# Pooling mixer of a two-layer decoder on one core: the two output tiles ahead of it, the mixer and the next squares as one list in an order kept by four engines

## Chip, cores and metric

The kernel runs on one core of a Trainium2 chip. The metric is the device time of one execution in microseconds (us), lower is better; it is given as the median of several runs. The engines are PE (TensorE, matmuls), DVE (VectorE), ACT (ScalarE), POOL (GpSimd) and SP (SyncE, which issues most loads).

## What is computed

One step of a decoder with two layers, for 512 prompt tokens and 8 sample tokens together (520 columns), all in float32, d_model 1024, d_ff 2816:

```python
x = x + 0.5 * swiglu(rms(x, g[l, 0]))           # every layer, first channel mixer
h = rms(x, g[l, 1])
x = x + (pool_mixer(h) if l == 0 else attention(h) @ w_o)
x = x + 0.5 * swiglu(rms(x, g[l, 2]))           # every layer, second channel mixer
y = rms(x, final_g)                             # at the end
```

The pooling mixer of layer 0 splits the 1024 features into four groups of 256. Group gi takes, for each token, the mean of the last 2, 4, 8 or 16 rows of h minus h itself, multiplies it by a 256x256 matrix and a scale per feature. The last 15 rows of h are outputs too (`pool_prompt`, `pool_sample`).

## The kernel before, in words

**Layout.** Features lie on the 128 partitions, tokens on the free axis: `x[k]`, k = 0 to 7, is 128x520. Every factor of a matmul is split into a rounded high part (by ACT, `hi`) and the rest (by DVE, `lo`), and each product is three matmuls: hi*hi, lo*hi, hi*lo. A split is thus always an ACT instruction, then a DVE instruction that reads its result.

**Weights.** `Weights` (L96) keeps a list of chunks (one DRAM load of up to 1 MB each on SP's queue into one of three `raw` buffers) and of items (a slice of a chunk, split into `wh`, `wl`, six buffers each). `get` hands out the next item, `prefetch` splits items five ahead. `hi` (L200) splits one item for a hand-written list: it returns `low`, the DVE half, and `ahead` (L219), which issues the load of the chunk two further on and then `add_up` for the next chunk. For a chunk that a Strassen tile uses, `add_up` calls `loaded` (L152): it loads a second copy `S` of 256 KB on SP and then starts two accumulating DMAs on POOL: `S<-raw` (L156), which needs `S` landed, and `raw<-raw` (L157). A new chunk can only be loaded when a `raw` buffer is free, that is when the last split of the chunk that held it is done. SP's loads are kept in the order of the program (`later`, L351).

**The channel mixer.** `ffn` (L672) computes hidden tiles, two plain ones (`plain_tile`, L577) and 20 by a Strassen scheme (`strassen_tile`, L614) in the case of the second one, and after each part of 8, 8 and 6 hidden tiles the eight output tiles m = 0 to 7. An output tile is 36 matmuls in the last part (`mm_tile`), `u` = result times 1/rms (DVE, L711), `x[m] -= u/2` (DVE, L712), and then, in the last part, `deferred` (L721): the split of g*x[m] for the next stage (xh, xl, L348 and L349), the square (ACT, L468) and its sum into `acc` (DVE, L472).

**The mixer** (L1006 to L1102). `zt(gi)` (L1013) multiplies the two feature tiles of a group by its matrix, in five parts tau: four blocks of 128 prompt tokens and one for the samples, six matmuls each. Parts 0 to 3 lie in one two-bank PSUM tile (`duo`, four such tiles exist), part 4 in another. `rstd_tok` (L477) sums `acc` over the partitions with five matmuls against a column of ones (L483) and computes 1/rms by 12 small DVE instructions (`root`, L486). `zt_evac` (L1031) takes every part out of PSUM, times 1/rms, as zh (ACT, L348) and zl (DVE, L349). `band` (L1038) multiplies zh, zl by the constant band matrices: 13 matmuls for each of the eight feature tiles m (L1052, L1060, L1061), then x[m] gets the result (L1062, L1065) and is split for the next channel mixer. The program is written as z0, norm, z1, evac 0, z2, evac 1, band 0, z3, evac 2, band 1, evac 3, band 2, band 3, then the eight squares and sums, then eight transposes for the 15 rows (L1095) and their copies (L1097). In what order the instructions go to the engines is decided by the framework's scheduler when the kernel is built.

**After it.** Behind the mixer, SP's queue has the copies of the state and of the caches (L1105, L1108: 0.4 and twice 1 MB) and 16 loads of sinks (L1114). The second `ffn` starts with two plain tiles; its `start_hooks` (L732) place `rstd_tok` behind the first of them and, around and after it, the combinations `sums` (L649) of g*x that the Strassen tiles need (xa, xb on ACT, L656; t on DVE, L661 to L667; th, tl, L345 and L346).

**Lists.** Three other stages (start, attention, end) are written as `Steps` (L237): each step has a name, an engine, an assumed cost, a due time, the steps it must follow (`after`), the buffers it takes (`takes`) and whose use frees them (`reads`). `order` plays the steps through: when an engine is free, the ready step with the earliest due time goes. The steps are emitted in the order of these start times inside `tc.manual_schedule`, which keeps that order on the engines named.

Of the kernel before, what the change touches and what calls it, by code (L numbers as in the profile page):

```python
# [18 lines left out]
P = 128  # L19
D = 1024  # L20
# [283 lines left out]
def yoco_step(ctx, tc, ins, outs):  # L304
# [27 lines left out]
    def ps():  # L332
        return duo()[:, 0, :]
# [117 lines left out]
        return gT[:, n * 8 + k : n * 8 + k + 1]  # L451

    N_KV, N_FIN, N_PS = 6, 7, 8
    r_tok = cp.tile([P, 8], F32, name="r_tok")
    R = cp.tile([P, TOK], F32, name="R")
    minus_half = cp.tile([P, 5], F32, name="minus_half")
# [9 lines left out]
    def square(k, pool, tag, order=lambda ins: ins):  # L466
        sq = pool.tile([P, TOK], F32, tag=tag, name="sq", bufs=1 if tag == "rp0" else 2)
        S.activation(sq, x[k], AF.Square)  # L468
        if k == 0:
            order(V.tensor_copy(acc[:, :TOK], sq))  # L470
        else:
            order(V.tensor_tensor(acc[:, :TOK], acc[:, :TOK], sq, op=ALU.add))  # L472
# [196 lines left out]
            split(tt[k + 4], t34)  # L669
            yield  # L670

    def ffn(fi, tmp, mov, hooks, tt, tags, after, before_last=None, given=None, end=None):  # L672

        j = 0
        for pi, n in enumerate(PARTS):
            last = pi == len(PARTS) - 1
            hs = Hidden(tags)
            for _ in range(n):
                if given is not None:
                    given(hs)  # L680
                    given = None
                elif j < NPL[fi]:
                    plain_tile(tmp, mov, hs, hooks)
                else:
# [8 lines left out]
            for m0 in range(0, KT, 2):  # L693
                banks = {m: duo() for m in (m0, m0 + 1)}
                if m0 == 0:
                    late = []
                    for m in (0, 1):
                        for k0, k1 in ((0, nk), (nk, n)):
                            w = W.get()
                            for k in range(k0, min(k1, n - 1)):  # L700
                                mm(w, k - k0, hs[k], banks[m], k == 0, False)
                            finish()
                        late.append((w, m))
                    for w, m in late:
                        mm(w, n - 1 - nk, hs[n - 1], banks[m], False, True)
                    W.prefetch()
                for m in (m0, m0 + 1):
                    if m0:
                        mm_tile(hs, banks[m])
                    u = tmp.tile([P, TOK], F32, tag="sb", name="u", bufs=nsb[0])  # L710
                    V.tensor_tensor(halves(u), banks[m][:, :, :H], halves(R), op=ALU.mult)  # L711
                    V.scalar_tensor_tensor(x[m], u, -0.5, x[m], op0=ALU.mult, op1=ALU.add)  # L712
                    if last:
                        if before_last is not None:
                            next(before_last, None)
                        after(m)

    def ff_pool():
        return tc.tile_pool(name="ff", bufs=2)

    def deferred(n, tmp, tag, tags, lst, w=TOK):  # L721


        def f(k):
            z = pair(tags, [P, w])
            split(tuple(a[:, :TOK] for a in z), x[k], gcol(n, k))
            lst.append(z)
            square(k, tmp, tag)

        return f  # L730
# [20 lines left out]
    with ff_pool() as tmp:  # L751
# [202 lines left out]
            return [step, norm, two, norm_all, two, step, step]  # L954

        prep = {}
        sel = cp.tile([P, 34], F32, name="sel")
        sts = cp.tile([P, KT, NS], F32, name="sts")

        def pool_prep():  # L960

# [44 lines left out]
    with tc.tile_pool(name="pm", bufs=2) as pm:  # L1006
        for k in range(KT):
            split(tuple(z[:, TOK:TW] for z in mov1[k]), sts[:, k, :])

        tok0 = (0, 128, 256, 384, 400)  # L1010
        r5 = pm.tile([P, 1], F32, name="r5", bufs=1)

        def zt(gi):  # L1013

            pd = duo()
            banks = [pd[:, 0, :], pd[:, 1, :], ps()]
            wh, wl = prep["w", gi]
            views = []
            for tau in range(5):
                o = banks[tau // 2][:, (tau % 2) * 256 : (tau % 2) * 256 + 256]  # L1020
                views.append(o)
                n = 0
                for kk in range(2):
                    xh, xl = mov1[2 * gi + kk]
                    s = slice(tok0[tau], tok0[tau] + P)
                    for a, b in ((xh, wh), (xh, wl), (xl, wh)):
                        T.matmul(o, a[:, s], b[:, kk, :], start=(n == 0), stop=(n == 5))  # L1027
                        n += 1
            return views

        def zt_evac(views):  # L1031
            zh = pm.tile([P, 5, 256], F32R, tag="zh", name="zh")
            zl = pm.tile([P, 5, 256], F32R, tag="zl", name="zl")
            for tau in range(5):
                split((zh[:, tau, :], zl[:, tau, :]), views[tau], r_tok[:, tau : tau + 1] if tau < 4 else r5)
            return zh, zl

        def band(gi, zz):  # L1038

            zh, zl = zz  # L1040
            Gt, (th, tl) = prep["G", gi], (prep["T", gi][:, 0, :], prep["T", gi][:, 1, :])
            G = lambda c: Gt[:, B_G + c : B_G + c + 256]
            for mi in range(2):
                m = 2 * gi + mi
                c = slice(mi * P, (mi + 1) * P)
                pd = duo()
                po, pso = pd[:, 0, :], pd[:, 1, :]
                pl = [(0, zh, th), (0, zl, th), (0, zh, tl), (1, zh, G(0)), (1, zl, G(0))]
                pr = [(1, zh, G(256)), (1, zl, G(256)), (2, zh, G(128)), (2, zl, G(128)), (3, zh, G(0)), (3, zl, G(0))]
                for half, lst in ((0, pl), (1, pr)):  # L1050
                    for i, (tau, z, b) in enumerate(lst):
                        T.matmul(  # L1052
                            po[:, half * 256 : half * 256 + 256],
                            z[:, tau, c],
                            b,
                            start=(i == 0),
                            stop=(i == len(lst) - 1),
                        )
                bs = Gt[:, B_S : B_S + NS]
                T.matmul(pso[:, :NS], zh[:, 4, c], bs, start=True, stop=False)  # L1060
                T.matmul(pso[:, :NS], zl[:, 4, c], bs, start=False, stop=True)  # L1061
                V.scalar_tensor_tensor(  # L1062
                    x[m][:, SP:], pso[:, :NS], gcol(N_PS, m), x[m][:, SP:], op0=ALU.mult, op1=ALU.add
                )
                V.scalar_tensor_tensor(  # L1065
                    x[m][:, :SP], po, gcol(N_PS, m), x[m][:, :SP], op0=ALU.mult, op1=ALU.add
                )
                z = pair(XX, [P, TOK])
                split(z, x[m], gcol(2, m))
                mov2.append(z)  # L1070

        mov2 = []
        hx = pm.tile([P, KT, P], F32, name="hx", bufs=1)
        for k in range(KT):
            S.activation(hx[:, k, 0:120], x[k][:, 400:520], AF.Copy, scale=gcol(1, k))
        z0 = zt(0)
        rstd_tok()
        z1 = zt(1)
        V.tensor_scalar(r5, r_tok[:, 4:5], sel[:, 32:33], sel[:, 33:34], op0=ALU.mult, op1=ALU.add)
        e0 = zt_evac(z0)  # L1080
        z2 = zt(2)
        e1 = zt_evac(z1)
        band(0, e0)
        z3 = zt(3)
        e2 = zt_evac(z2)
        band(1, e1)
        e3 = zt_evac(z3)
        band(2, e2)
        band(3, e3)
        for m in range(KT):  # L1090
            square(m, pm, "sq", later)
        for a in range(2):
            pt = ps()
            for k in range(4):
                T.transpose(pt[:120, k * P : (k + 1) * P], hx[:, a * 4 + k, 0:120], ident)  # L1095
            hrow = splp.tile([120, 512], F32, tag="S", name="hrow", bufs=4)
            S.activation(hrow, pt[:120, :], AF.Copy, scale=r_tok[:120, 4:5])  # L1097
            cols = slice(a * 512, (a + 1) * 512)
            nc.gpsimd.dma_start(pool_prompt[0, 0, :, cols], hrow[97:112, :])
            nc.gpsimd.dma_start(pool_sample[0, :, 14, cols], hrow[112:120, :])  # L1100

    movk = []  # L1102
    with ff_pool() as tmp:
# [853 lines left out]
```

## Time and profile before

| | us |
|---|---|
| three runs, median (lowest to highest) | 1675.85 (1675.25 to 1677.2) |
| the profiled execution | 1674.63 |
| its span, from the first to the last instruction | 1672.9 |

PE is busy in 98% of the span, DVE in 75%, ACT in 53%, POOL in 10%. The profile gives times within the span in us from its start; the mixer lies between 377 and 411. L-numbers are lines of the kernel; a name such as `ps` or `raw` stands for all its buffers. Matmul rows overlap: a matmul of 256 columns is shown with about 0.28 us, and one starts every 0.12 us.

### The profile page before, as it was taken

The numbers are of one execution on the slowest core, as the hardware profiler recorded it, in microseconds if no ns is written. First come the engines' busy times: TensorE is split into PE (matmuls) and PEld (weight loads), VectorE is DVE, ScalarE is ACT, GpSimd is POOL, SyncE is SP. The second block draws the span as 40 slices with busy tenths as digits, with TensorE's granted clock in tenths as the row PEclk, the third lists the DMA queues.
The fourth block names the chain that finished last, engine by engine and source line by source line (L and its number), as shares of the span: only waits on it lengthen the run. The fifth ranks groups of instructions, "written<-read, shape, count | busy, mean of one in ns | idle before, by whom it ended". The sixth has DMA issues, their size and how long they took to land.

```text
span 1672.9 us, 34562 instructions
## 1 busy us (share of the span) xinstructions
PE 1643.2 (98%) x13802; PEld 1625.0 (97%) x13802; DVE 1253.7 (75%) x2400; ACT 883.9 (53%) x1763; POOL 175.3 (10%) x235
## 2 busy tenths in 40 slices
PE   9899999999899999999999999999999999999997
PEld 9899999998899999999999999999989999999997
DVE  6865875887885785779785785778997785785786
ACT  6643643665662562556462463455875663463463
POOL 1101101100100100100110110100220110110100
PEclk9999999999999999999999999999999999999999
DMA  9446846653466666643765665644142575665641
GB/s 241 101 134 138 177 139 139 164 170 109 94 149 161 139 152 164 139 115 92 168 152 156 141 159 147 145 136 122 41 97 61 119 168 143 146 166 135 140 118 52
DMA packets 318240, 227.08 MB, mean 136 GB/s; under 512 B 9568, under 2 KB 293336, under 8 KB 318038
## 3 DMA queue, kind: packets, MB, share of 16 engines
q1 hardware_dynamic: 291360, 178.50, 38.1%
q0 software_dynamic: 23392, 41.83, 15.5%
q10 hardware_dynamic: 3326, 4.53, 0.9%
q8 instruction: 108, 1.77, 0.4%
q14 instruction: 54, 0.44, 0.1%
HBM read 180.89 MB, written 5.04 MB: 111 GB/s over the span
## 4 chain that ended last, share of the span: by engine, by line
PE 93%; DVE 4%; ACT 1%; issue 1%; DMA 0%; DVEq 0%; POOL 0%; ACTq 0%
PE ps L545 47%; PE ps L519 33%; PE pa L519 5%; PE ps L1778 2%; PE p L519 1%; PE pb L1383 1%; PE pc L1454 1%; PE pc L1439 1%; PE ps L1027 1%; DVE wl L193 1%; PE ps L1052 1%; DMA S<-raw 0%; DVE tl L346 0%; PE t L809 0%; ACT wh L192 0%
## 5 line engine op out<-in xcount | busy, mean ns | idle before, releaser
L192 ACT ACTIVATE wh<-raw 128x512 fp32r<-128x512 f32 (+1 forms) x690 | 418.2, 622 | 509.9 <-PE ps L519 295.0
L193 DVE TENSOR_TENSOR wl<-raw,wh 128x512 fp32r<-128x512 f32 (+1 forms) x690 | 456.4, 677 | 188.1 <-ACT wh L192 183.9
L545 PE MATMUL ps<-th,wh 128*128 128x260 f32 x1264 | 358.7, 284 | 4.1 <-ACT th L345 1.7
L545 PE MATMUL ps<-tl,wh 128*128 128x260 f32 x1264 | 358.1, 284 | 0.6 <-DVE tl L346 0.6
L545 PE MATMUL ps<-th,wl 128*128 128x260 f32 x1264 | 356.4, 284 | 1.0 <-DVE wl L193 1.0
L545 PEld LDWEIGHTS ps<-th,wh 128*128 128x128 f32 x1264 | 239.0, 189 | 5.6 <-ACT th L345 2.1
L545 PEld LDWEIGHTS ps<-tl,wh 128*128 128x128 f32 x1264 | 239.0, 189 | 1.0 <-DVE tl L346 1.0
L545 PEld LDWEIGHTS ps<-th,wl 128*128 128x128 f32 x1264 | 238.3, 189 | 1.5 <-DVE wl L193 1.5
L519 PE MATMUL ps<-hh,wh 128*128 128x260 f32 x1024 | 206.9, 283 | 0.6 <-ACT vtok L1205 0.6
L519 PE MATMUL ps<-hl,wh 128*128 128x260 f32 x1024 | 207.4, 283 | 0.0
L519 PE MATMUL ps<-hh,wl 128*128 128x260 f32 x1024 | 205.4, 282 | 0.0
L545 PE MATMUL ps<-xh,wh 128*128 128x260 f32 x708 | 199.6, 284 | 4.3 <-ACT wh L192 3.8
L545 PE MATMUL ps<-xl,wh 128*128 128x260 f32 x708 | 198.9, 283 | 0.0
L157 POOL DMA_DIRECT2D raw<-raw x79 | 68.4, 866 | 1242.1 <-DVE wl L193 556.3
L545 PE MATMUL ps<-xh,wl 128*128 128x260 f32 x708 | 195.4, 283 | 1.4 <-DVE wl L193 1.4
L519 PEld LDWEIGHTS ps<-hl,wh 128*128 128x128 f32 x1024 | 158.5, 189 | 0.0
L519 PEld LDWEIGHTS ps<-hh,wh 128*128 128x128 f32 x1024 | 157.1, 188 | 0.9 <-ACT vtok L1205 0.9
L519 PEld LDWEIGHTS ps<-hh,wl 128*128 128x128 f32 x1024 | 157.4, 188 | 0.0
L545 PEld LDWEIGHTS ps<-xh,wh 128*128 128x128 f32 x708 | 133.9, 189 | 5.2 <-ACT wh L192 4.4
L711 DVE TENSOR_TENSOR u<-ps,R 128x520 f32<-128x520 f32 x88 | 61.2, 696 | 98.4 <-PE ps L519 98.4
L545 PEld LDWEIGHTS ps<-xl,wh 128*128 128x128 f32 x708 | 134.0, 189 | 0.0
L545 PEld LDWEIGHTS ps<-xh,wl 128*128 128x128 f32 x708 | 131.9, 189 | 1.8 <-DVE wl L193 1.8
(299 smaller groups left out, 3241.3 us busy)
## 6 DMA issues: line engine op xcount, KB each, us to landing
raw<-in_ffn_w_gate_dram SPq DMA_DIRECT2D x87, 512.0 KB
raw<-in_ffn_w_up_dram SPq DMA_DIRECT2D x87, 512.0 KB
raw<-in_ffn_w_down_dram SPq DMA_DIRECT2D x32, 1024.0 KB
raw<-raw POOLq DMA_DIRECT2D x79, 256.0 KB, 3.3
S<-in_ffn_w_up_dram SPq DMA_DIRECT2D x79, 256.0 KB
S<-raw POOLq DMA_DIRECT2D x79, 256.0 KB, 4.7
raw<-in_ffn_w_down_dram SPq DMA_DIRECT2D x16, 768.0 KB
raw<-in_w_q_dram SPq DMA_DIRECT2D x8, 512.0 KB
```

What stands on the lines that cost most here:

```text
L157: G.dma_start(blk(raw, 2, 1), blk(raw, 1, 1), accum_op=ALU.add)
L192: nc.scalar.activation(dh, src, AF.Copy)
L193: nc.vector.tensor_tensor(dl, src, dh.bitcast(F32), op=ALU.subtract)
L519: T.matmul(banks[:, hf, :H], a[:, kk, :], hcols(b, hf), start=(first and i == 0), stop=(last and i == 2),)
L545: T.matmul(bank[:, :H], a[:, kk, :], b, start=(not more and kk == 0 and i == 0), stop=(kk == 3 and i == 2), skip_group_check=more,)
L711: V.tensor_tensor(halves(u), banks[m][:, :, :H], halves(R), op=ALU.mult)
L1027: T.matmul(o, a[:, s], b[:, kk, :], start=(n == 0), stop=(n == 5))
L1052: T.matmul(po[:, half * 256 : half * 256 + 256], z[:, tau, c], b, start=(i == 0), stop=(i == len(lst) - 1),)
L1383: T.matmul(o, q_[rows_, qc], k_[rows_, kc_], start=(i == 0), stop=(i == 2))
L1439: T.transpose(pt[:, o : o + P], vals["sm", t, h, bi][:, e, kt * P : (kt + 1) * P], ident)
L1454: T.matmul(po[rows_, bi * P : (bi + 1) * P], vtok[:, max(b - 1, 0) + kt, v0 : v0 + 64], vals["pp", t, h, bi][:, kt * 256 + e * P : kt * 25 ...
L1778: T.matmul(bank, a[:, k % 3, :], b[:, c0:c1], start=(k == 0 and i == 0), stop=(k == 5 and i == 2))
```

## The change

The first `ffn` stops after output tile 5 (`stop=6`). Output tiles 6 and 7, their splits, the mixer, its norm, the splits for the second channel mixer, the squares and sums for its norm and the transposes become one list of steps. `manual_schedule` names PE, DVE, ACT and POOL.

- The steps of `pool_prep` that went with output tiles 6 and 7 go, two each, with tiles 4 and 5. `sel` and `sts` are allocated earlier; the split of `sts` goes with each tile.
- The square of x[7] is no longer added to `acc` on DVE: `norm_sums` has ten matmuls in place of five (each column: `acc`, then the square). The 12 DVE instructions of `root` become one (`norm_mean`) and a power on POOL (`norm_root`).
- In the list, z0 to z2 are due ahead of the evacuations. The fifth parts of groups 0 and 1 share one bank of the tile in which the norm's sums are, those of groups 2 and 3 one bank of another tile.
- zh and zl lie in four pairs of 128x2x256 tiles of the hidden tiles' pool, one for parts 0 and 1 and one for 2 and 3, and small ones for part 4.
- Each band puts its halves into two banks and the samples beside the first; the result is added to x[m] by two DVE instructions as before.
- Items 0 to 8 of the weights are in the list (0 to 3 for output tiles 6 and 7, 4 to 7 the first hidden tile of the second `ffn`, 8 the first quarter of the second); five of them are split before the list begins.

The core of the diff:

```diff
-        ffn(0, tmp, mov0, first_hooks(), tt, HH, deferred(1, tmp, "g", XX, mov1, TW), pool_prep(), first_tile)
+        hs0 = ffn(0, tmp, mov0, first_hooks(), tt, HH, deferred(1, tmp, "g", XX, mov1, TW), pool_prep(), first_tile, stop=6)
+    with tc.tile_pool(name="pm", bufs=2, reuse_waits="tile") as pm:
+        first = W.ng
+        have = W.ns - first
+        st = Steps(dict(d=4, w=6, sq=2, u=2))
...
+        def w_lo(i):
+            lows.pop(i)()
+            aheads.pop(i)()
+
+        add("x5", "DVE", 3.0, -100.0)
+        add("y5", "ACT", 2.5, -100.0)
...
+        W_DUE = (0, 0, 2, 4, 33, 34, 37, 38, 42)
+        for i in range(9):
...
+                add(f"wh{i}", "ACT", 0.13 * n + 0.13, W_DUE[i], lambda i=i: w_hi(i), after=prev, takes=("w",))
+                add(f"wl{i}", "DVE", 0.14 * n + 0.13, W_DUE[i] + 0.1, lambda i=i: w_lo(i), after=[f"wh{i}"])
...
+            if n == 1 and m == 7:
+                nc.gpsimd.memset(q[:, TOK:], 0.0)
...
+                T.matmul(o, acc[:, lo : lo + P], ones[:, 0:1], start=True, stop=False)
+                T.matmul(o, vals["q", 1, 7][:, lo : lo + P], ones[:, 0:1], start=False, stop=True)
...
+        def norm_root():
+            nc.gpsimd.tensor_tensor(r_tok[:, :5], v, minus_half, op=ALU.pow)
...
+        def z_bank(gi, tau):
+            if tau < 4:
+                return vals["z", gi][:, tau // 2, (tau % 2) * 256 : (tau % 2) * 256 + 256]
+            return vals["f", gi // 2][:, 0, (gi % 2) * 256 : (gi % 2) * 256 + 256]
...
+            add(f"u{m}", "DVE", 0.7, d, lambda m=m: upd(m), after=[f"o{m}1"], takes=("u",), reads=[("d", f"o{m}0")])
+            add(f"x{m}", "DVE", 0.7, d + 0.1, lambda m=m: add_u(m), after=[f"u{m}"], reads=[("u", f"u{m}")])
...
+        for k in range(KT):
+            add(f"hx{k}", "ACT", 0.3, 9.0 + 0.1 * k, lambda k=k: h_part(k), after=[f"x{k}"] if k > 5 else ["y5"])
+        add("ns", "PE", 1.25, 10.5, norm_sums, after=["q7", "a6"], takes=("d",), reads=[("sq", "q7")])
+        add("nm", "DVE", 0.17, 11.0, norm_mean, after=["ns"], reads=[("d", "ns")])
+        add("nr", "POOL", 1.4, 11.0, norm_root, after=["nm"])
+        add("n5", "DVE", 0.28, 12.0, norm_r5, after=["nr"])
+
+        Z_DUE = (8.7, 12.3, 16.2, 19.5)
+        E_DUE = (13.5, 16.5, 19.5, 22.5)
+        B_DUE = lambda m: 23.5 + 1.8 * m
...
+                    f"eh{gi}{tau}", "ACT", 0.48, e, lambda gi=gi, tau=tau: z_hi(gi, tau),
+                    after=[f"z{gi}{tau}", "nr" if tau < 4 else "n5"] + first_e,
...
+                    f"ez{gi}{tau}", "DVE", 0.49, e + 0.5, lambda gi=gi, tau=tau: z_lo(gi, tau),
+                    after=[f"eh{gi}{tau}"], reads=[("d", holder)],
...
+            add(f"xp{m}", "DVE", 0.74, d + 1.5, lambda m=m: x_prompt_(m), after=[f"b{m}0", f"b{m}1", f"hx{m}"], reads=[("d", f"b{m}0")])
+            add(f"yh{m}", "ACT", 0.72, d + 2.3, lambda m=m: y_hi(m), after=[f"xs{m}", f"xp{m}"] + ([f"yh{m - 1}"] if m else []))
+            add(f"yl{m}", "DVE", 0.76, d + 3, lambda m=m: y_lo(m), after=[f"yh{m}"])
+            add(f"sq{m}", "ACT", 0.63, d + 12, lambda m=m: sq_of(2, m), after=[f"xs{m}", f"xp{m}", "ns"], takes=("sq",))
...
+        add("ht", "PE", 0.95, 30.0, h_turn, after=[f"hx{k}" for k in range(KT)], takes=("d",))
...
+        with tc.manual_schedule(
+            engines={mybir.EngineType.PE, mybir.EngineType.DVE, mybir.EngineType.Activation, mybir.EngineType.Pool}
+        ):
+            st.emit()
+        W.ng = first + 4
```

Steps are named o (output tile), u, x, q (square), a (sum), h and l (split of g*x), sh and sl (split of `sts`), ns, nm, nr, n5 (the norm), z (product of a group), eh and ez (its evacuation), b (band), xs and xp (result into x), yh and yl (split for the next channel mixer), sq and sa (square and sum for its norm), ht and ho (transposes and their copies), wh and wl (split of a weight item).

## Rows read from the trace of the kernel before

**Rows 1.** The page: span, busy shares, and the chain that ended last by engine.

```profile
span 1672.9 us, 34562 instructions
PE 1643.2 (98%) x13802; PEld 1625.0 (97%) x13802; DVE 1253.7 (75%) x2400; ACT 883.9 (53%) x1763; POOL 175.3 (10%) x235
PE 93%; DVE 4%; ACT 1%; issue 1%; DMA 0%; DVEq 0%; POOL 0%; ACTq 0%
```

**Rows 2.** Stretches: length; busy PE, PEld, DVE, ACT, POOL; granted clock; DMA share; GB/s.

```profile
378.00:384.00 6.00, 3.85 (x35) 3.68 (x33) 4.06 (x8) 2.59 (x7) 0.70 (x1) 1.00 1.03 296
386.00:388.00 2.00, 2.00 (x11) 2.00 (x11) 1.57 (x7) 1.05 (x3) 0.00 (x0) 0.50 0.91 295
437.00:450.00 13.00, 7.99 (x51) 6.33 (x50) 11.15 (x23) 8.77 (x17) 0.00 (x0) 1.00 0.01 2
```

**Rows 3.** Waits of PE, 360 to 452: us in total, times, longest.

```profile
PE ps L483 <- DVE acc L472: 2.2, 1, 2.2
PE ps L1052 <- DVE x L1065: 1.1, 1, 1.1
```

**Rows 4.** Chain of waits by time: start, us, what.

```profile
383.00 1.25 PE ps L483 x10
...
403.71 1.37 PE ps L1052 x11
...
405.20 1.35 PE ps L1052 x11
...
411.61 11.68 PE ps L519 x96
```

**Rows 5.** Timeline of PE: first and 24th matmul of z0.

```profile
377.13 0.29 PE L1027 MATMUL ps<-th,xh 128*128 128x256 f32 x1
...
379.87 0.28 PE L1027 MATMUL ps<-th,xl 128*128 128x256 f32 x1
```

**Rows 6.** Timeline of DVE, 359 to 428.

```profile
359.15 0.75 DVE L346 TENSOR_TENSOR bt<-pr,bt 128x256 fp32r<-128x256 f32 x2
...
371.85 0.68 DVE L712 SCALAR_TENSOR_TENSOR x<-u,x 128x520 f32<-128x520 f32 x1
...
376.24 1.28 DVE L193 TENSOR_TENSOR wl<-raw,wh 128x512 fp32r<-128x512 f32 x2
377.44 0.74 DVE L349 SCALAR_TENSOR_TENSOR xl<-x,gT,xh 128x520 fp32r<-128x520 f32 x1
378.11 0.68 DVE L711 TENSOR_TENSOR u<-ps,R 128x520 f32<-128x520 f32 x1
378.72 0.68 DVE L472 TENSOR_TENSOR acc<-acc,sq 128x520 f32<-128x520 f32 x1
...
386.50 0.17 DVE L498 SCALAR_TENSOR_TENSOR r_tok<-nt,ny 128x5 f32<-128x5 f32 x1
...
424.34 0.17 DVE L491 TENSOR_SCALAR nv<-ps 128x5 f32<-128x5 f32 x1 [1.57 <-PE ps L483]
```

**Rows 7.** Timeline of ACT: evacuation of group 2.

```profile
396.48 0.45 ACT L348 ACTIVATE zh<-ps,r_tok 128x256 fp32r<-128x256 f32 x1
396.83 0.46 ACT L348 ACTIVATE zh<-ps,r 128x256 fp32r<-128x256 f32 x1
...
398.34 0.47 ACT L348 ACTIVATE zh<-ps,r_tok 128x256 fp32r<-128x256 f32 x1
399.35 0.47 ACT L348 ACTIVATE zh<-ps,r_tok 128x256 fp32r<-128x256 f32 x1 [0.55 <-DVE zl L349]
400.38 0.47 ACT L348 ACTIVATE zh<-ps,r_tok 128x256 fp32r<-128x256 f32 x1 [0.55 <-DVE zl L349]
```

**Rows 8.** Timelines of SP and POOL, 376 to 386.

```profile
376.94 0.37 SPq L359 DMA_DIRECT2D raw<-in_ffn_w_gate_dram  x1
...
377.98 1.03 SPq L359 DMA_DIRECT2D S<-in_ffn_w_up_dram  x1
...
384.83 0.86 POOL L156 DMA_DIRECT2D S<-raw  x1 [0.67 <-DMA sink_s<-in_attn_sinks_dram]
```

**Rows 9.** The power on POOL in the last stage: ns min/median/max.

```profile
L1851 POOL TENSOR_TENSOR r_tok<-nv,minus_half x3: 543/696/1092, 1646.6 to 1666.1; 128x2 f32<-128x2 f32 x2, 8x1 f32<-8x1 f32 x1
```

More of the change, by code (lines that the diff above doesn't have):

```diff
@@ L670, in sums, with ffn @@
             yield
-    def ffn(fi, tmp, mov, hooks, tt, tags, after, before_last=None, given=None, end=None):
+    def ffn(fi, tmp, mov, hooks, tt, tags, after, before_last=None, given=None, end=None, stop=KT):
         j = 0
@@ L692, in ffn @@
                 break
-            for m0 in range(0, KT, 2):
+            for m0 in range(0, stop if last else KT, 2):
                 banks = {m: duo() for m in (m0, m0 + 1)}
@@ L715, in ffn @@
                             next(before_last, None)
+                            if stop < KT and m >= stop - 2:
+                                next(before_last, None)
                         after(m)
+        return hs
     def ff_pool():
@@ L1031, in zt_evac, with w_hi @@
[L1031 to L1040, printed above, removed]
+        hx = pm.tile([P, KT, P], F32, name="hx", bufs=1)
+        v = cp.tile([P, 5], F32, tag="nv", name="nv")
+        def w_hi(i):
+            lows[i], aheads[i] = W.hi()
@@ new lines, in out, with upd, add_u @@
+        def out(m, h):
+            if h == 0:
+                vals["o", m] = duo()
+            w = W.items[first + 2 * (m - 6) + h][2]
+            for k in range(3 * h, 3 * h + 3):
+                mm(w, k - 3 * h, hs0[k], vals["o", m], k == 0, k == 5)
+        def upd(m):
+            vals["u", m] = u = pm.tile([P, TOK], F32, tag="u", name="u")
+            V.tensor_tensor(halves(u), vals["o", m][:, :, :H], halves(R), op=ALU.mult)
+        def add_u(m):
+            V.scalar_tensor_tensor(x[m], vals["u", m], -0.5, x[m], op0=ALU.mult, op1=ALU.add)
@@ new lines, in z_part @@
+        def z_part(gi, tau):
+            if tau == 0:
+                vals["z", gi] = duo()
+            if gi == 2 and tau == 4:
+                vals["f", 1] = duo()
+            o = z_bank(gi, tau)
+            wh, wl = prep["w", gi]
+            n = 0
+            for kk in range(2):
+                xh, xl = mov1[2 * gi + kk]
+                s = slice(tok0[tau], tok0[tau] + P)
+                for a, b in ((xh, wh), (xh, wl), (xl, wh)):
+                    T.matmul(o, a[:, s], b[:, kk, :], start=(n == 0), stop=(n == 5))
+                    n += 1
@@ L1041, in band @@
+        def band(m, part):
+            gi, c = m // 2, slice((m % 2) * P, (m % 2 + 1) * P)
+            zh, zl = 0, 1
             Gt, (th, tl) = prep["G", gi], (prep["T", gi][:, 0, :], prep["T", gi][:, 1, :])
             G = lambda c: Gt[:, B_G + c : B_G + c + 256]
[L1043 to L1058, printed above, removed]
-                bs = Gt[:, B_S : B_S + NS]
[L1060 to L1070, printed above, removed]
@@ L1087, in yoco_step @@
[L1087 to L1095, printed above, removed]
+            if part == 0:
+                vals["b", m] = duo()
+                lst = [(0, zh, th), (0, zl, th), (0, zh, tl), (1, zh, G(0)), (1, zl, G(0))]
+            elif part == 1:
+                lst = [(1, zh, G(256)), (1, zl, G(256)), (2, zh, G(128)), (2, zl, G(128)), (3, zh, G(0)), (3, zl, G(0))]
+            else:
+                bs = Gt[:, B_S : B_S + NS]
+                lst = [(4, zh, bs), (4, zl, bs)]
@@ L1100, in yoco_step @@
             nc.gpsimd.dma_start(pool_sample[0, :, 14, cols], hrow[112:120, :])
+        for m in (6, 7):
+            d = 4.35 * (m - 6)
+            for h in range(2):
+                i = 2 * (m - 6) + h
+                before = [f"o{m}0"] if h else ["o61"] if m == 7 else []
+                add(
+                    f"o{m}{h}", "PE", 2.17, d + 2.17 * h, lambda m=m, h=h: out(m, h), after=[f"wl{i}"] + before,
+                    takes=() if h else ("d",), reads=[("w", f"wh{i}")],
+                )
+            d += 4.4
+            add(f"u{m}", "DVE", 0.7, d, lambda m=m: upd(m), after=[f"o{m}1"], takes=("u",), reads=[("d", f"o{m}0")])
+            add(f"x{m}", "DVE", 0.7, d + 0.1, lambda m=m: add_u(m), after=[f"u{m}"], reads=[("u", f"u{m}")])
+            late = 0.0 if m == 7 else 1.0
+            add(f"q{m}", "ACT", 0.63, d + 0.2 + late, lambda m=m: sq_of(1, m), after=[f"x{m}"], takes=("sq",))
+            if m == 6:
+                add("a6", "DVE", 0.7, d + 1.5, lambda: sum_of(1, 6), after=["q6", "x5"], reads=[("sq", "q6")])
+            add(f"h{m}", "ACT", 0.73, d + 0.5, lambda m=m: x_hi(m), after=[f"x{m}", "y5"])
+            add(f"l{m}", "DVE", 0.76, d + 1.0, lambda m=m: x_lo(m), after=[f"h{m}"])
+            add(f"sh{m}", "ACT", 0.19, d + 3, lambda m=m: s_hi(m), after=[f"h{m}"])
+            add(f"sl{m}", "DVE", 0.16, d + 3, lambda m=m: s_lo(m), after=[f"sh{m}"])
@@ new lines, in yoco_step @@
+        for k in range(KT):
+            add(f"hx{k}", "ACT", 0.3, 9.0 + 0.1 * k, lambda k=k: h_part(k), after=[f"x{k}"] if k > 5 else ["y5"])
[5 more added lines that the diff above has]
+        E_DUE = (13.5, 16.5, 19.5, 22.5)
@@ L1102, in yoco_step @@
+        add("ht", "PE", 0.95, 30.0, h_turn, after=[f"hx{k}" for k in range(KT)], takes=("d",))
+        for a in range(2):
+            add(f"ho{a}", "ACT", 0.6, 32.0, lambda a=a: h_out(a), after=["ht", "nr"], reads=[("d", "ht")])
+        with tc.manual_schedule(
[3 more added lines that the diff above has]
+        W.ng = first + 4
     movk = []
```

148 lines of the change are left out of this document (113 added, 35 removed).

## The prediction

> **What bounds the kernel now.** I read the page first. PE is busy in 98% of the span and carries 93% of the chain that ended last [rows 1]: time is gained only where PE stands still or runs slowly. The waits of PE around the mixer show where: 2.2 us for the last sum into `acc` before the norm, and 1.1 us in the bands for a result on DVE [rows 3]. Of the stretches, 378 to 384 has PE busy for 3.85 of 6 us, and 386 to 388 ran at a granted clock of 0.50, 1.2 GHz in place of 2.4, after that pause and the one-column matmuls of the norm [rows 2]. The chain gives the ends: the norm's matmuls begin at 383.0, the second channel mixer at 411.6 [rows 4]. The next stall is in 437 to 450, PE busy 7.99 of 13 while DVE is busy 11.15 [rows 2]; there the Strassen operands bind.
>
> The sum is made against the profiled execution: 1674.63 us, of which the span is 1672.9, 1.73 lying around it; the median of the runs, 1675.85, is 1.2 above it. From no change a measurement of this kernel tells 0.2%, 3.35 us.
>
> **The head of the list.** On PE, tiles 6 and 7 and then z0 stay where they are. Played through with its own costs, the list sends parts 0 to 3 of z0, then the norm's matmuls, z1, both fifth parts, z2, z3, the fifth parts of 2 and 3, the bands. A part is six matmuls at 0.119 us (24 from 377.13 to 379.87 [rows 5]), 0.71, so z0's four are done at 380.0.
>
> DVE, in order: x[5] ends at 372.5; after ACT's 0.73 follow its xl and sum, as in [rows 6], where an addition goes every 0.61 us (378.11 to 378.72) and an xl every 0.67 (377.44 to 378.11). That is 373.3 + 0.67 + 0.61 + 0.1 = 374.7. The list's order is then u6, x6, two weight splits (four times 0.61), xl6, a6 and a small one (1.36): 378.5; u7, x7: 379.7. The square (ACT, 0.6) ends at 380.4. PE waits 0.4 where it waited 2.2. Ten matmuls at 1.25/5 [rows 4] take 2.5, to 382.9: 1.25 more than before. The mean (0.17, as L491 [rows 6], and its latency) ends at 383.2. The power was 0.54 to 1.09 us on at most two columns [rows 9]; for five I take the upper one (bounds 0.7 and 1.4): **1/rms at 384.3 against 386.67** [rows 6].
>
> The moved steps of `pool_prep` cost nothing: the last ran at 359.15 [rows 6], long ahead of tile 4's end. The eight copies hx fill ACT's gaps before x6.
>
> **What stands ahead of the power on POOL.** `ahead` of item 8 issues the Strassen chunk B on SP and, for chunk A, the load of S and two accumulating DMAs on POOL. In the list's own play wl7 and wl8 go right behind x7, 2 us ahead of the power, and POOL is one of the engines whose order is kept. So POOL has: the small memset, `S<-raw`, `raw<-raw`, then the power; and behind the power wait all 20 evacuations on ACT.
>
> `S<-raw` waits for S to land. Before, B was issued at 376.94, just as wl7 ended (the first of two at 376.24), S at 377.98, and `S<-raw` could start at 384.83 [rows 8], 7.9 us after B's issue. Nobody waited for it: 1/rms was on DVE. Now wl7 ends at 379.7 + 0.6 = 380.3, B follows, and the same queue behind it (S, then the copies of state and caches) gives 380.3 + 7.9 = 388.2. Two DMAs of 0.86 [rows 8] and the power: **1/rms at 388.2 + 1.7 + 1.1 = 391.0**, 4.3 later than before. From below: wl7 cannot end before tile 7's last matmul (377.1), two additions and itself, 379.0; with S landing 6.85 after that (what S took from its own issue, as if B ahead of it cost nothing), the same two DMAs and the power in 0.7, 1/rms is at 388.3. From above, x7 a microsecond later and the power at 1.4: 392.3. I take 391.0, nearest to the measured queue. The state copies and sink loads behind it on SP shift by 3.4 us too; the next load on SP comes far later, so that costs nothing.
>
> **The evacuations.** In group 2, zh of a part starts 1.03 us after the previous part's (399.35, 400.38), each having waited for that part's zl; the fifth part went 0.35 after the first [rows 7]. So parts 0 to 3 of a group, in one two-bank tile, go one by one. The list assumes 0.48 per part and puts one group after the other on ACT, so four groups take 4 times (3 x 1.03 + 2 x 0.35) = 15.2 us, where the scheduler had two groups interleaved.
>
> The Trainium skill, page "PSUM — Partial Sum Buffer", section "PSUM bank collisions raise a hardware error", says that two engines have to be kept apart only on one bank and quadrant. By it part 2 would not wait for part 1 and the sum would be 2.8 us shorter; the trace disagrees, since part 2 (399.35), the first in its bank, waited 0.55 for part 1's zl [rows 7].
>
> **PE behind the norm.** z1, two fifth parts and z2 are ten parts, 382.9 + 7.1 = 390.0. z3 takes z0's tile, free when that is evacuated: 391.0 + 3.1 + 1.0 = 395.1. PE stands 5 us (if the clock falls behind the norm as before, that is hidden in it). Then z3, the fifth parts and bands 0 and 1 run to about 403; half clock after the pause can cost 2 us there, hidden behind the next wait: band 2 takes z3's tile, whose last evacuation ends at 391.0 + 3 x 3.8 - 0.35 + 3.1 + 1.0 = 406.1. Six bands at 1.49 (403.71 to 405.20 [rows 4]) and eight transposes at about 0.14: 406.1 + 8.9 + 1.1 = **416.1 against 411.6: 4.5 us later.** DVE after its last zl (407): x and yl of a band cost 0.15 + 0.66 + 0.67 = 1.5, PE's pace, so it keeps up, and the 1.1 us wait for x in the bands [rows 3] has no place of its own; the eight sums come last, 419 + 4.9 = 424, before PE asks for them at 416.1 + 11.7 = 428.
>
> **Downstream.** The first half of the next mixer is the same work. Before, DVE idled 1.57 us before that norm [rows 6]; now it idles more, and some Strassen sums may be pulled forward, shortening the stall in 437 to 450 by 0 to 1.5; a second drop of the clock may cost 0 to 1.7. I let the two cancel. **Sum: +4.5**, 1679.1 by the profiled execution, and on the median **1680.4**.
>
> **Rivals.**
> - *POOL is free* (the two DMAs do not stand ahead of the power, or S lands early; then that part of the list does what it says): 1/rms at 384.3, z3's last evacuation at 399.4, the second mixer at 409.4, 2.2 earlier: 1673.7; with sums pulled forward down to 1671. For it: before, `S<-raw` stood in nobody's way, and POOL is 10% busy [rows 1]. Against: the list keeps POOL's order, and wl8's place in it is early. It decides where S lands before 383.
> - *The stall swallows it*: the Strassen sums need x alone, so if they are put ahead of the norm, PE comes 5 us later to a stall of 5.0 us that has not moved: 1676. Against: before they ran behind the norm although x was there.
> - *Evacuation by banks*: only parts 1 and 3 wait, so a group takes 0.7 less, 2.8 in four; 1/rms still late: +4.5 - 2.8 = +1.7, 1677.6. Against: part 2's wait [rows 7].
>
> **Numbers.** Forecast 0.52 (+2 to +7.5: slower by over 0.2% in 0.42, within in 0.10). POOL free 0.25 (faster 0.13, within 0.12). Stall swallows 0.10, banks 0.08, both within. Another order elsewhere in the program, 0.05: faster 0.02, slower 0.03. Together faster 0.15, same 0.40, slower 0.45. The range leaves out a tenth below, in POOL free, and a tenth above, in the late landings: 1672.2 to 1683.4. The forecast's own is 1677.9 to 1683.4.
>
> **What would show it.** In the new trace: `S<-raw` on POOL between the memset and the power, the power's start after 387, the first zh 4 us later than 386.8; zh 1.03 apart; PE idle ahead of z3 and band 2; the second mixer's first matmul near 416. A power that starts at 383 proves the forecast wrong; zh 0.5 apart proves its second half wrong.

## The result, and the profile after

The changed kernel takes **1681.4 us** (median of 7 runs, 1679.32 to 1687.52) against 1675.85 of the kernel before: a ratio of 1.0044, 95% interval [1.0031, 1.0057], so slower by more than a measurement can miss. The ratio weighs all runs and is not the quotient of the two medians, which is 1.0033; two of the seven runs lie at 1686.71 and 1687.52. The profiled execution took 1681.4, 6.8 us more than that of before.

The page of the changed kernel, to be read against [rows 1]: span, busy shares, the chain that ended last by engine.

```profile
span 1679.6 us, 34572 instructions
PE 1645.9 (98%) x13812; PEld 1627.9 (97%) x13812; DVE 1251.2 (74%) x2388; ACT 883.7 (53%) x1763; POOL 177.9 (11%) x237
PE 89%; DVE 5%; ACT 3%; DMA 2%; issue 1%; SPq 0%; POOL 0%; DVEq 0%; ACTq 0%
```

The span is 6.7 us longer, and PE's share of the chain fell from 93% to 89%: DVE, ACT and DMA got it. Where, the chain of waits shows, cut to the steps that matter (start, us, what):

```profile
380.41 0.71 DVE x L1059
...
381.14 0.65 ACT sq L1078
...
382.82 1.22 SPq L359
...
386.42 2.63 DMA sraw<-in_attn_sinks_dram
389.04 0.07 POOL S L156
389.12 0.49 issue
389.61 1.26 POOL raw L157
390.87 1.25 POOL r_tok L1101
392.12 0.02 issue
392.14 0.85 ACT hh L1135 x2
...
401.90 3.81 PE ps L1123 x18
405.71 5.99 PE ps L1159 x52
411.70 0.95 PE ps L1184 x8
412.64 5.99 PE ps L1159 x52
418.63 1.43 PE ps L521 x11
```

The second channel mixer begins at 418.63 instead of 411.61 [rows 4], 7.0 us later, and that is all of the loss: from there to the end of the span it is 1261.0 us, before 1261.3. PE is not in this chain between 376 and 401.9; DVE, loads, POOL and the evacuations are.

POOL's timeline between the memset (361.52) and the power:

```profile
388.23 0.86 POOL L157 DMA_DIRECT2D raw<-raw  x1 [26.60 <-DMA sink_s<-in_attn_sinks_dram]
389.03 0.95 POOL L156 DMA_DIRECT2D S<-raw  x1
389.61 1.26 POOL L157 DMA_DIRECT2D raw<-raw  x1
390.18 1.93 POOL L1101 TENSOR_TENSOR r_tok<-nv,minus_half 128x5 f32<-128x5 f32 x1
```

SP's timeline, chunk B and S:

```profile
381.78 0.37 SPq L359 DMA_DIRECT2D raw<-in_ffn_w_gate_dram  x1
...
382.82 1.22 SPq L359 DMA_DIRECT2D S<-in_ffn_w_up_dram  x1
```

This is the picture of the forecast, with one DMA more: ahead of the power stand not only the two sums of chunk A but first `raw<-raw` of chunk B, which the scheduler had moved forward from behind the list. It needs B itself, and starts 6.45 us after B's issue; the mean had been there since 384.2. The name in brackets is the last DMA seen, a small load of sinks. That POOL waited for B is read from the times: in runs 1, 7 and 8 this DMA starts 6.33 to 6.37 us after B's issue, and before it was 6.36 (376.94 [rows 8] to 383.30). For it stood in the trace of before too, ahead of `S<-raw` at 384.83, in a row that [rows 8] leave out:

```profile
383.30 0.86 POOL L157 DMA_DIRECT2D raw<-raw  x1 [8.66 <-DMA sink_s<-in_attn_sinks_dram]
```

PE's waits from 376 to 420 (total, times, longest), against [rows 3]:

```profile
PE ps L1123 <- DVE hl L1139: 3.3, 1, 3.3
PE ps L1123 <- ACT hh L1135: 1.7, 1, 1.7
PE ps L1095 <- ACT sq L1078: 1.6, 1, 1.6
PE ps L1094 <- DVE xl L1074: 0.3, 1, 0.3
```

ACT's timeline, group 0 and the first two parts of group 1:

```profile
392.14 0.84 ACT L1135 ACTIVATE hh<-ps,r_tok 128x256 fp32r<-128x256 f32 x2 [9.36 <-POOL r_tok L1101]
393.53 0.48 ACT L1135 ACTIVATE hh<-ps,r_tok 128x256 fp32r<-128x256 f32 x1 [0.55 <-DVE hl L1139]
394.56 0.47 ACT L1135 ACTIVATE hh<-ps,r_tok 128x256 fp32r<-128x256 f32 x1 [0.55 <-DVE hl L1139]
...
395.29 0.84 ACT L1135 ACTIVATE hh<-ps,r_tok 128x256 fp32r<-128x256 f32 x2
```

Stretches of the changed kernel (columns as in [rows 2]):

```profile
378.00:384.00 6.00, 4.01 (x34) 3.75 (x33) 5.31 (x10) 3.88 (x10) 0.00 (x0) 1.00 0.15 40
386.00:388.00 2.00, 2.00 (x11) 2.00 (x11) 0.00 (x0) 0.00 (x0) 0.00 (x0) 0.50 1.48 449
396.00:404.00 8.00, 6.30 (x28) 6.00 (x29) 4.22 (x10) 3.90 (x10) 0.00 (x0) 0.50 0.45 111
444.00:457.00 13.00, 8.01 (x50) 6.36 (x49) 11.09 (x21) 8.26 (x16) 0.00 (x0) 0.97 0.01 2
```

The norm's stretch is no better than before, the first half clock (386 to 388, 1.2 GHz) is as before, and there is a second one, behind the wait ahead of z3, eight microseconds long. The stall of the Strassen operands is the same 8.01 of 13 us as before, only 7 us later.

From the first matmul of z0 to the second mixer it was 34.5 us before (377.13 to 411.61) and is 42.2 now (376.48 to 418.63), 7.7 more. PE's waits are 6.9 against 3.5 us: +3.4. Ten matmuls for the norm took 2.25 (nine starts from 381.83 to 383.86, and one earlier) against 1.1: +1.1. Half clock lost (length times one less the granted clock, in stretches of 2 us from 384 to 406, without the idle time) about 5.4 against 1.7: +3.7. That makes 8.2 for 7.7 measured, which is as near as such sums come.

### The profile page after: what moved, and what is told of

It is laid out like the page before. It is cut to its first block, busy times and chain, and to the rows that moved or that the text cites. A ratio compares the mean times of both kernels' runs of the same rounds, so it can differ in the third digit from the quotient of the medians.

```text
span 1679.6 us, 34572 instructions
## 1 busy us (share of the span) xinstructions
PE 1645.9 (98%) x13812; PEld 1627.9 (97%) x13812; DVE 1251.2 (74%) x2388; ACT 883.7 (53%) x1763; POOL 177.9 (11%) x237
## 3 DMA queue, kind: packets, MB, share of 16 engines
q1 hardware_dynamic: 291360, 178.50, 38.3%
## 4 chain that ended last, share of the span: by engine, by line
PE 89%; DVE 5%; ACT 3%; DMA 2%; issue 1%; SPq 0%; POOL 0%; DVEq 0%; ACTq 0%
PE ps L547 46%; PE ps L521 31%; PE pa L521 5%; PE ps L1947 2%; PE pb L1552 1%; PE pc L1623 1%; PE pc L1608 1%; PE ps L1159 1%; DMA pr<-in_bands_dram 1%; DVE wl L193 1%; DVE tl L346 0%; DMA S<-in_ffn_w_up_dram 0%; DMA S<-raw 0%; DMA raw<-in_ffn_w_gate_dram 0%; ACT wh L192 0%
```

## The experiments

All ten are built from the changed kernel. Runs 1 to 4, 5 to 8, and 9 and 10 form three groups, each on another chip. The runs of one group shared the runs of the kernel before, which had a median of 1674.83, 1674.79 and 1674.83 in the three groups; the ratios are to those, and that of the changed kernel is to the 1675.85 above. Times are medians; a trace is of one execution, and can lie a few microseconds from its kernel's median.

The first matmul of z0 lies between 375.0 and 377.4 in these traces, and the memset, far ahead of all that the edits touch, differs alike (359.6 to 362.4). So the last column, the time from z0 to the second mixer, compares traces better than the second mixer's own time; for the kernel before it is 34.5. From the second mixer to the end it is 1260.8 to 1263.2 us in every trace but that of run 10, where it is 1265.1.

| run | us | ratio [95%] | first evacuation | second mixer | z0 to it |
|---|---|---|---|---|---|
| changed kernel | 1681.4 | 1.0044 [1.0031, 1.0057] | 392.1 | 418.6 | 42.2 |
| power ahead of the sums | 1680.5 | 1.0029 [1.0018, 1.0039] | 385.8 | 414.6 | 38.3 |
| root on DVE | 1677.7 | 1.0007 [0.9996, 1.0019] | 386.2 | 410.1 | 35.1 |
| power ahead, groups in turns | 1676.8 | 1.0011 [1.0001, 1.0021] | 385.7 | 412.6 | 35.4 |
| root on DVE, groups in turns | 1677.0 | 1.0009 [0.9999, 1.0020] | 388.9 | 415.8 | 38.4 |
| reads behind the fourth part | 1679.6 | 1.0030 [1.0019, 1.0041] | 390.7 | 414.4 | 39.1 |
| both: power ahead, reads behind | 1675.2 | 1.0008 [0.9996, 1.0019] | 385.2 | 409.9 | 33.4 |
| these, norm behind z1, batches | **1671.8** | **0.9985 [0.9976, 0.9993]** | 386.5 | 407.5 | 31.4 |
| the same, power behind the sums | 1680.4 | 1.0033 [1.0020, 1.0045] | 391.9 | 414.5 | 38.1 |
| norm behind z1, no batches | 1675.4 | 1.0001 [0.9989, 1.0012] | 386.6 | 410.4 | 34.0 |
| batches, norm ahead of z1 | 1677.3 | 1.0009 [0.9997, 1.0021] | 387.5 | 412.6 | 35.2 |

**1. The power ahead of the three sums.**

```diff
 def w_lo(i):
     lows.pop(i)()
-    aheads.pop(i)()
+    if i != 8:
+        aheads.pop(i)()
...
+add("wa8", "-", 0.0, 12.0, lambda: aheads.pop(8)(), after=["nr", "wl8"])
```

> Edit: the changed kernel with the ahead part of weight split 8 (the two Strassen sums of chunk A, and with them the sum of chunk B that had come in ahead of them) made a step of the list that follows the power, so that the GpSimd queue runs memset, power, then the three sums. Nothing else moves; the loads of chunk B stay where they are in SyncE's order. Theory (the power is late only because it stands behind three accumulating DMAs that wait for chunk B and S to land): the mean at 384.04 us is followed by the power at once, 1/rms is there at 384.3 + 1.3 to 1.9 = 385.6 to 386.2 instead of 392.1, z3's tile is free before z2 is done (392.6), so the 3.3 us of idle ahead of z3 and the 1.7 us behind its third part go; the next mixer's first matmul comes at 410.5 to 413 instead of 418.6, and the time is 1673.5 to 1676 (the kernel before: 1675.85). Rival A (the list itself, with its evacuation chain of 3.2 us a group and bands behind all of z, costs the time): 1/rms comes early, but the next mixer still starts at 416 or later, time 1679 or more. Rival B (the stall at 444 to 457 waits for a load of fixed time, so an earlier start is swallowed there): next mixer by 413, idle from 444 to 457 grows from 5 to 10 us or more, time 1679 or more.

POOL's timeline, then two of PE's waits:

```profile
384.55 1.19 POOL L1102 TENSOR_TENSOR r_tok<-nv,minus_half 128x5 f32<-128x5 f32 x1 [23.53 <-DVE nv L1099]
387.54 0.92 POOL L157 DMA_DIRECT2D raw<-raw  x1 [1.81 <-DMA sink_s<-in_attn_sinks_dram]
```
```profile
PE ps L1124 <- ACT hh L1136: 2.0, 1, 2.0
PE ps L1096 <- ACT sq L1079: 1.6, 1, 1.6
```

The power follows the mean at once, 1/rms is there at 385.7, 6.4 us earlier, and the 3.3 us of idle ahead of z3 are gone: the queue was the cause of both. But the second mixer gained only 4.0 of them (414.6, where 410.5 to 413 was expected) and the time stayed at 1680.5. The half of the theory by which nothing else holds PE fell. Rival A's time came true, though its second mixer at 416 or later did not; and a piece of its cause was in plain sight, a wait of 2.0 us for ACT in the middle of z3, which the changed kernel also has, with 1.7. Rival B is out: PE is idle for 3.7 us of 440 to 453, not for 10. Of the 4.0 us this trace lost 2.2 again behind the second mixer (1263.2 us to the end against 1261.0); why stays open.

**2. The root on DVE.** The power replaced by the instructions of `root`, in the list at 2.3 us on DVE; POOL keeps its three sums where they are.

```diff
-nc.gpsimd.tensor_tensor(r_tok[:, :5], v, minus_half, op=ALU.pow)
+V.tensor_scalar(y.bitcast(I32), v.bitcast(I32), 1, None, op0=ALU.arith_shift_right)
...
-add("nr", "POOL", 1.4, 11.0, norm_root, after=["nm"])
+add("nr", "DVE", 2.3, 11.0, norm_root, after=["nm"])
```

> Edit: the changed kernel with the power on GpSimd replaced by the eleven small VectorE instructions that the kernel before used (shift, subtract, three Newton steps), in the same place of the list; the GpSimd queue keeps its three sums where they are. Theory (queue behind the sums): 1/rms is there 2.4 us behind the mean, as in the kernel before (384.28 to 386.67), so at 386.5; first evacuation on ScalarE at 386.8; no wait ahead of z3; next mixer's first matmul 411.5 to 414, time 1674.5 to 1677, about 1 us behind the run that only reorders the queue. Rival A (the list itself): next mixer 416 or later, 1679 or more. Rival C (the power is slow in itself, whatever stands ahead of it): this run reaches 1676 and the reordered queue does not.

1/rms came 2.4 us behind the mean (383.76 to 386.2) and the second mixer at 410.1, earlier than expected, but z0 began 1.5 us earlier too, so that from z0 it is what was expected; the traced execution took 1673.12, the median was 1677.7, a little above the range. By the order of the two times alone rival C would fit. The traces speak against it: in the first run the power took 1.19 us, and 1/rms was there 1.2 us behind the mean's end, sooner than here. What made this run better is the list: with 2.3 us assumed for the root, `order` put group 3's reads behind z3's fourth part, that part carries no wait for ACT any more, and PE stands still nowhere inside z3. That led to run 5.

**3 and 4. Evacuations of two groups in turns**, with the power ahead and with the root on DVE.

```diff
-E_DUE = (13.5, 16.5, 19.5, 22.5)
+E_DUE = (13.5, 13.75, 19.5, 19.75)
```

> Edit: the reordered queue of the first run, and the evacuations of groups 0 and 1, and of groups 2 and 3, ordered in turns (part 0 of group 0, part 0 of group 1, part 1 of group 0, ...) by their due times, so that consecutive evacuations read different two-bank tiles. Theory that the split of a part (ScalarE's high half, then VectorE's low half) is serialised inside a tile, 1.03 us a part where 0.84 us for two were seen: the twenty evacuations take about 10.5 to 11 us instead of 13; but from 386 on TensorE has z1's rest, z2, z3 and the bands in front of it without a gap, so at most 0 to 1.5 us of it shows: next mixer 409.5 to 412, time 1673 to 1675.5. Rival D (evacuations are not on the path at all once 1/rms is early): same as the first run within 0.2%, and no row of TensorE waits for hl or hh.

> Edit: the VectorE root of the second run with the evacuations in turns of the third. Theory: as the second run, less what the turns take off the path: 1673.5 to 1676. Rival D: as the second run within 0.2%.

Neither reached its range (1676.8 and 1677.0). The evacuations did get shorter: in run 3 the last nine parts of groups 0 and 1 left from 388.69 to 392.91, 0.47 each. But with these due times the third and the fourth part of z3 both wait for a read of the tile, and PE stood still twice in the mixer after the norm, 2.0 us (run 3) and 1.7 us (run 4) in all. Run 4 is level with run 2, as rival D has it, and run 3 is faster than run 1. The two runs don't tell the theories apart, because the due times changed more than one thing.

**5. Reads only behind the fourth part**, with POOL as the change has it.

```diff
-after=[f"z{gi}{tau}", "nr" if tau < 4 else "n5"] + first_e,
+after=[f"z{gi}{max(tau, 3)}", "nr" if tau < 4 else "n5"] + first_e,
```

> Edit: the changed kernel with one more condition in its list: a part of a group is read by ScalarE only after the fourth part of that group is written (the first run still had TensorE waiting 2.01 us for ScalarE's hh in the middle of z3, at 397.8, where z3's fourth part is issued behind reads of the same two-bank tile; the changed kernel waits 1.70 us there). The power stays behind the three sums, so 1/rms stays at about 392. Theory (second cause: TensorE's write into a tile waits for earlier reads of another part of that tile): the wait of 1.70 us goes, z3 to z34 run as 36 matmuls without a gap from 396.0, and the next mixer starts 2 to 3.5 us earlier, at 415 to 416.6, time 1677.5 to 1679.5. Rival (the wait only moves to the next evacuation, so the order of reads is indifferent): next mixer at 418 or later, time 1680 or more.

PE's only wait from 386 to 404 in its timeline:

```profile
394.54 0.58 PE L1123 MATMUL ps<-th,xh 128*128 128x256 f32 x1 [3.35 <-DVE hl L1139]
```

The 1.7 us inside z3 are gone, those ahead of z3 stay: the second cause is real and separate. In the program the fourth part of z3 carries a wait on ACT, because in the changed list a read of another part of the same two-bank tile comes earlier; with the new condition that wait is not there. From z0 to the second mixer it took 3.1 us less, within the 2 to 3.5 expected; the time, 1679.6, is at the upper end of its range. The ratio went from 1.0044 to 1.0030, a step that the two intervals do not tell from none.

**6. Both at once.**

> Edit: both at once, the power ahead of the three sums (first run) and the reads of a group behind its fourth part. Theory (two causes, the queue and the order inside z3, that hid each other: the first run took 1/rms from 392.1 to 385.7 and the next mixer only from 418.5 to 414.5, with 2.01 us of wait inside z3): no wait of TensorE inside z3, next mixer 410.5 to 412.5, time 1673.5 to 1676, that is, no slower than the kernel before. Rival (TensorE's half clock, 382.3 to 389 in the first run, is what is left, and sets it): next mixer 413 or later, time 1677 or more.

Nothing waits inside z3, the second mixer starts at 409.9, a little earlier than expected, 1675.2: level with the kernel before. Of the way from z0 the first cause alone gave 3.8 us, the second 3.1, both together 8.8. By the ratios it is 0.0015, 0.0014 and 0.0036, of which only the last is clear of noise. The half clock ahead of it (0.50 at 384 to 386) did not keep it from that, so the rival is out as the thing that is left; it is still a cost, as run 10 shows.

**7. The norm's sums behind four parts of z1, and evacuation in batches.**

```diff
-add("ns", "PE", 1.25, 10.5, norm_sums, after=["q7", "a6"], ...)
+add("ns", "PE", 1.25, 10.5, norm_sums, after=["q7", "a6", "z13"], ...)
...
-    after=[f"eh{gi}{tau}"], reads=[("d", holder)],
+    after=[f"eh{gi}{max(tau, 3)}"], reads=[("d", holder)],
```

> Edit: as the second of this call, and the sums of the norm follow the first four parts of z1 (TensorE stood idle for 1.64 us behind the first sum, waiting for the square), and VectorE's low halves of a group follow all four high halves of it, so that ScalarE and VectorE read different tiles. Theory: no idle time on TensorE between z0 and the bands but up to 1 us ahead of z3; if the half clock at 382 to 389 came from that idle time, it goes with it; bands from about 394, next mixer 407 to 410, time 1669 to 1673, 0.1 to 0.3% below the kernel before. Rival (the clock falls whatever TensorE does there): half clock stays at 382 to 389, next mixer 410 to 412, time 1673 to 1675.5.

ACT's timeline (first two groups), PE's waits, and two stretches:

```profile
386.48 1.57 ACT L1136 ACTIVATE hh<-ps,r_tok 128x256 fp32r<-128x256 f32 x4 [4.24 <-POOL r_tok L1102]
387.92 0.49 ACT L1136 ACTIVATE zh<-ps,r 128x256 fp32r<-128x256 f32 x1
388.28 1.60 ACT L1136 ACTIVATE hh<-ps,r_tok 128x256 fp32r<-128x256 f32 x4
```
```profile
PE ps L1124 <- DVE hl L1140: 0.8, 1, 0.8
PE ps L1124 <- DVE nv L1099: 0.3, 1, 0.3
```
```profile
378.00:384.00 6.00, 6.00 (x55) 6.00 (x54) 5.08 (x10) 3.33 (x9) 0.00 (x0) 1.00 0.25 70
384.00:388.00 4.00, 3.75 (x31) 3.55 (x31) 0.44 (x2) 1.52 (x5) 1.63 (x2) 1.00 1.19 340
```

Four parts leave in 1.6 us, a group in 1.8, PE stands still for 1.0 us in all from z0 to the second mixer, and in this trace it is at full clock all that way: the second mixer at 407.5, 4.1 us ahead of the kernel before (3.1 counted from z0), **1671.8 us, ratio 0.9985**. This beats both kernels. That the clock stays up because the idle time is gone, as the theory has it, is not shown: it fell in runs 8 and 9, which have the norm in the same place.

**8. The same with the power behind the sums.**

> Edit: the third of this call with the power put back behind the three sums, as the change has it. Theory (the queue costs what it delays 1/rms by, once nothing else holds z3): 1/rms at about 392, TensorE idle for 5 to 7 us ahead of z3 and at half clock behind it, next mixer 413.5 to 416, 5 to 8 us behind the third run; time 1676 to 1679. Rival (the list's order alone made the change slow): within 2 us of the third run.

One wait of PE, one stretch:

```profile
PE ps L1123 <- DVE hl L1139: 4.6, 1, 4.6
```
```profile
384.00:388.00 4.00, 3.74 (x22) 3.55 (x22) 0.17 (x1) 0.00 (x0) 0.00 (x0) 0.64 1.30 376
```

This is the cleanest pair: one step of the list apart, 414.5 against 407.5 (6.7 us counted from z0), and 8.6 us apart by the medians (ratio 1.0033 against 0.9985). The time, 1680.4, is above the range given. In a list in which nothing else holds z3, the queue costs 7 us of the way to the second mixer. The clock differs too: here it fell at 385, in run 7 it did not, though PE's work up to there is the same.

**9 and 10. The two halves of run 7 apart.**

> Edit: the run that beat both kernels (1671.78 us) with VectorE's low halves put back in turns with ScalarE's high halves; the power is ahead of the three sums and the norm's sums follow four parts of z1. Theory: in turns a group takes ScalarE 3.2 us, with batches 1.8 us (first groups 386.48 to 388.28), so group 3 is read some 4 us later; the third band waits for it, and the next mixer starts 1 to 2.5 us later than 407.39, at 408.5 to 410, time 1673 to 1674.5. Rival (the order of the evacuation does not show, the norm's place alone gave the gain): next mixer within 0.5 us of 407.39, time within 0.5 us of 1671.78.

> Edit: the run that beat both kernels with the norm's sums put back ahead of z1; the power is ahead of the three sums and the evacuations stay in batches. Theory: TensorE stands idle for 1.64 us behind the first sum again, and the half clock behind it costs 1.5 us more as in the run with the queue and the whole tiles (382 to 388); bands no earlier than 396, next mixer 409 to 410, time 1673.5 to 1675.5. Rival (what is idle ahead of 1/rms is covered, the evacuation alone gave the gain): next mixer within 0.5 us of 407.39.

Without batches (run 9) the second mixer starts at 410.4, 2.9 later (2.7 from z0; a little more than expected), and what waits is the third band. PE's timeline, and a stretch:

```profile
400.28 0.36 PE L1160 MATMUL ps<-bt,hh 128*128 128x256 f32 x1 [1.65 <-DVE x L1163]
```
```profile
386.00:388.00 2.00, 2.00 (x13) 2.00 (x12) 0.76 (x2) 0.84 (x2) 0.78 (x2) 0.53 1.30 407
```

DVE's last low half of z3's parts ended at 400.14, and the small x that the profile names went right behind it; PE's work follows both. The half clock of that trace lies ahead of this wait, which hides it: from 386 to 400 no evacuation of ACT waits for a matmul. Without the move of the norm (run 10) it is 412.6 (3.9 later from z0), later than expected: PE waits 1.64 us for the square and runs at half clock for the 4 us that follow it, and for two more, to 390. The traced execution was one of the longer ones, 1679.88 where the median is 1677.3. The stretch:

```profile
384.00:388.00 4.00, 4.00 (x20) 4.00 (x21) 0.93 (x4) 0.47 (x2) 1.19 (x1) 0.50 1.11 288
```

Both rivals are out: each half is needed for the time of run 7. The medians, 1675.4 and 1677.3 against 1671.8, lie above what was expected too.

## Why the prediction was right, and where not

Sign and chief mechanism were right: 1680.4 forecast, 1681.4 measured. The size was too low: +4.5 forecast, against +5.6 by the medians, +6.7 by the two spans and +7.0 at the second mixer, and that the medians lie 1 us apart is partly luck. A range from 1672.2 to 1683.4, which holds a gain as well as a loss, was easy to meet; what the traces bear out are the steps. By these:

- **The queue ahead of the power: right, with a DMA missed.** The forecast had two DMAs ahead of the power, the trace three. B was issued at 381.78 (forecast 380.3), since x7 came at 381.1 and not at 379.7; `S<-raw` then started 7.25 us after it (forecast 7.9), the first DMA at 388.23 (forecast 388.2, as it happens). 1/rms came at 392.1 against 391.0: B was 1.5 later, `S<-raw` 0.65 sooner behind it, and from `S<-raw` to 1/rms it was 3.1 where 2.8 was forecast. What the third DMA cost no run shows, for none takes it out. The power itself is 1.19 us where POOL is free (run 1), 1.25 in the chain here: the 1.1 taken was near. Runs 1, 2 and 8 show that this wait, and not the power, delays 1/rms.
- **PE's wait for the norm: wrong.** 0.4 us was forecast, 1.64 came, and 0.34 ahead of it for the last sum; the square of x7 was 1.4 later, for DVE's queue ran longer than the sum of its rows said. Ten matmuls took 2.25, forecast 2.5.
- **Evacuation one part at a time, 3.8 us a group: too dear.** The first two parts of a group went together (0.84 us for both), so a group took 3.2. The third part did wait 0.55 for DVE, as in [rows 7], and it is the first in its bank. Run 7 shows how the two go together: with all of ACT's reads of a two-bank tile ahead of DVE's, none of parts 0 to 3 waits for DVE. What waits is thus an order between reads of one tile that the program carries, not two engines at one bank. The Trainium skill, page "PSUM — Partial Sum Buffer", section "PSUM bank collisions raise a hardware error", has two engines kept apart only on one bank and quadrant. The 0.55 us do not speak against that, as the forecast had it, because they come from the program's order.
- **PE idle ahead of z3: right** in place and kind: z3 began at 396.0 (forecast 395.1). The wait itself was 3.3 us and not 5, since z2 ended 2.7 later than forecast.
- **Band 2 waits for z3's tile, and hides the half clock: wrong.** No band waited. In its place stand a wait of 1.70 inside z3 that the forecast did not have (runs 5 and 6), and half clock from 396 to 404. The wait inside z3 hides the first part of it; behind 401.9 nothing does, and 18 matmuls took 3.81 us there, where at 0.119 each it would be 2.1. That is why it became +7.0 and not +4.5.
- **Downstream neutral: right**, 1261.0 against 1261.3 us from the second mixer to the end. Neither of the two effects that it let cancel is seen there: the stall kept its length (PE busy 8.01 of 13 us against 7.99), at a clock of 0.97.

Of the rivals, *POOL is free* did not hold for this kernel, and its price was wrong: with the queue free and all else kept (run 1) the time was 1680.5, not 1673.7. It left out the wait inside z3 and the dearer norm; with those removed too (run 7) the kernel comes to where that rival put it. *The stall swallows it* is out, since the stall moved along whole. *Evacuation by banks* is out as a mechanism by the 0.55 us ahead of the third part, though its price, 0.7 us less a group, came near the 0.6 measured.

## What to carry to other kernels

Ask of every instruction put on an engine that also issues DMAs what stands ahead of it in that queue and what that waits for: the power took 1.2 us and cost 7 where nothing else held PE, and moving one step behind it got them back. After that, look for the waits that are left: here four orders (queue, reads inside a tile, the norm's place, batches) had to be set right for a gain of 0.15%, and with the first, the third or the fourth put back (runs 8, 10 and 9) the kernel was no faster than the one before. The second was not put back by itself. In a list written by hand, finish writing a PSUM tile before any engine reads it, and let one engine finish with a tile before the other begins.

## What the runs showed of the hardware that was not expected

- The clock of TensorE. In run 7 it stayed at 1.00 from 378 to 406; in run 8, with the same work up to 385.4 and a wait of 0.26 us there in both, it was at 0.50 (1.2 GHz) by 386. Run 9 has the same work and wait up to there once more, and its clock fell as well, to 0.53 from 386 to 388. So the full clock of run 7's trace may be the luck of one execution. A matmul of 256 columns starts every 0.213 us at 0.50 instead of 0.119. In the other traces a pause of 1.6 to 2.2 us and the one-column matmuls of the norm went ahead of the first fall, but runs 8 and 9 show that no such pause is needed for one; what decides was not tried and stays open.
- The scatter. The kernel before ranged from 1672.87 to 1676.84 over 23 runs beside run 7 (which ranged from 1670.56 to 1675.76 over 11), and from 1672.60 to 1681.67 over 23 beside runs 9 and 10. Whether the falls of the clock make the scatter wasn't tried, but the two go together: of the 78 executions of the kernel before in the three groups, the 24 with a mean granted clock of 0.994 or more took 1674.4 us on average, the 11 with 0.991 or less 1677.7.
- The same power took 1.93 us in the trace right behind three DMAs and 1.19 with nothing ahead of it; of the 1.93, the chain counts 1.25 as its own.
